# Moving transposes and gate products to later places in TensorE's queue: two layers of a diffusion trunk on one core

## The chip, the core and the metric

The kernel runs on one core of a Trainium2 chip. The metric is the device time of one execution, in microseconds; a change is judged by the median of several executions on the same chip. TensorE is written PE below (PEld for its weight loads), VectorE DVE, ScalarE ACT, GpSimd POOL and SyncE SP.

## What is computed

Two transformer layers over 512 latent tokens and 128 context tokens of width 1024, all in float32. The part of the reference that matters:

```python
def _layer(x, mod, p, lam_init, ctx):
    sh1, sc1, g1, sh2, sc2, g2 = mod
    h = _rmsnorm(x, p['norm1']) * (1.0 + sc1) + sh1
    m, new_ctx = _mixer(h, p, lam_init, ctx)
    x = x + g1 * m
    h = _rmsnorm(x, p['norm2']) * (1.0 + sc2) + sh2
    x = x + g2 * _conv_ffn(h, p)
    return x, new_ctx
```

The mixer projects h once and divides the columns among a bidirectional gated recurrence (RG-LRU, whose gates r and i are block products of the convolved input), grouped-query attention (q and k normalised per head, then rotated) and differential attention. Context tokens attend to context alone; latent tokens attend to the cached context keys and to themselves. The outputs are joined and projected back.

## The kernel before

**Tiling.** The 640 tokens are five tiles of 128: t = 0 to 3 latent, t = 4 context. Every float32 product is three products of rounded parts (mm3, L363 to L366: high by high, low by high, high by low), so one step over two k-blocks of one token tile is six matmuls. A layer runs: mixer (two LRU column blocks, then three projection groups `proj_group`, L633, of 4 weight blocks c times 5 token tiles; then the LRU gate columns), attention, output projection (`out_proj`), `ffn`.

**Who sets the order.** The schedule is manual: each engine gets its instructions in the order in which the Python program emits them. Work beside the products is put in by a small planner, `Flow` (L56). `fl.add(delay, fn, dve, need)` registers a function with a due time on the planner's own clock; `fl.step(ns)`, called after each step of products (1296 for a token tile of a group, 816 for two k-blocks of `stat_mm`), moves that clock and calls everything that is due, earliest due first. Some functions move the clock themselves (`fl.now += ...`) for the TensorE work that they put in. An item with a DVE cost is held while the planner's estimate of VectorE's backlog is over 1500, and an item with `need` waits for a free slot. These clock units are constants of the code, not measured times.

```python
GD = (5000, 1200, 11000, 2000)
CX = (3000, 4000, 4000, 3000, 6000, 12000, 8000)
NP = (1250, 4000, 950, 1700)
GQ = (5150, 3150, 2200, 1400)
```

**Queries.** `evac_gq` (L831), for each token tile of the first group: s1 (sums for the norm), s2 (scale and rotary, VectorE), s2b (rounding on GpSimd; needs one of two "st" slots), s3 (low part, L858, DVE), s4 (four transposes of a half into one PSUM bank, L867, and ScalarE's copies `qa`, L869; gives the slot back). The context tile takes c2 (L876) and c3 (four transposes `cqT`, L884). Key tiles take `k_stack` (L890): it needs an "st" slot too, and its `tr` (L902) puts in three transposes `kT`.

**Context attention.** `ctx_stage(n)` (L1049): four small score products `cS` (L1039) into two banks for n = 0, 1; row maxima on DVE (`cnm`, L1041); four exponentials on ACT (`cP`, L1044), which are the last readers of the two banks. Then `ctx_norm` and `ctx_T` (L1071, transposes `cPTp`). Stage 0 is due 12000 after the start of the third group, stage 1 20000 after it. The counter `pending["a"]` starts at 17 and falls with each s4 (8), key stack (5) and `ctx_T` (4); attention starts when it is 0.

**LRU gates.** `lru_gate` (L714): 16 products `gacc` (L722) for four calls, each followed by a sigmoid on ACT; due from 5000 on. They read xc, written by the convolution on DVE (L693, L696), and `lru_tail` (ACT, POOL, DVE) follows them.

**PSUM.** Outside attention there is one pool of eight banks (`pb`, L273). A bank goes to the next tile in the order in which banks were let go, and a tile that gets a used bank makes PE wait for the last reader of the old one. While a projection group runs, five banks hold its accumulators (one per token tile, `acc`), so that three go round among all transposes and small products.

**Norms.** `norm_pipe(t)` (L1323) is called as each tile of `out_proj` or `ffn` is finished: a (L1329: squares on ACT, then r and the scaled halves `xn` on POOL), 4000 later b (eight transposes `nT`, L569, into two banks, then `norm_c`: scale and shift on DVE and ACT, rounding `hi`, low part `lo`). The next stage starts with products over tiles 0 to 2 alone (384 columns, two weight blocks m of four pairs of k-blocks each), behind `need_h(0, 1, 2)` (L602), then goes on with tiles 3 and 4 (256 columns) behind `need_h(3, 4)`. There are three such joints: first out_proj to first ffn, first ffn to second mixer, second out_proj to second ffn.

Of the kernel before, what the change touches and what calls it, by code (L numbers as in the profile page):

```python
# [33 lines left out]
GD = (5000, 1200, 11000, 2000)  # L34
# [14 lines left out]
GQ = (5150, 3150, 2200, 1400)  # L49


def f32(ap):
    return ap.bitcast(F32)
# [179 lines left out]
def hybrid_kernel(ctx: ExitStack, tc: tile.TileContext, i, o):  # L233
# [13 lines left out]
    fl = Flow()  # L247
    fl.free["st"] = 2

    def half(name, dt=F32):  # L250
        return hpool.tile([128, 2 * W], dt, tag="h", name=name)

    def v2(t, n=W):
        return t.rearrange("p (a b) -> p a b", a=2)[:, :, :n]

    def tslot(name, n=644, dt=F32):
        return tp.tile([128, 644], dt, tag="t", name=name)[:, :n]
# [15 lines left out]
    def pb(name, dt=F32):  # L273
        return mode["pb"].tile([128, 512], dt, tag="pb", name=name)

    def pb2(name, cut=CH):

        return [pb(name), pb(name), cut]

    def small(name, n=8):  # L280
        return smp.tile([128, 8], F32, tag="sm", name=name)[:, :n]
# [86 lines left out]
    def round_pool(out, in_):  # L368
        pool.tensor_scalar(out=out, in0=in_, scalar1=1.0, scalar2=0.0, op0=ALU.mult, op1=ALU.add)
# [196 lines left out]
    def norm_b(n):  # L566
        pt = pb2("nT")
        for k in range(KD):
            pe.transpose(pt[k // 4][:, k % 4 * 128:k % 4 * 128 + 128], n[k // 4][:, k % 4 * 128:k % 4 * 128 + 128], ident)  # L569
        return pt  # L570
# [26 lines left out]
        fl.add(NP[2], hi)  # L597
        fl.add(NP[3], lo, 1340)

    h_left = set()  # L600

    def need_h(*tiles):  # L602
        while any(t in h_left for t in tiles):
            fl.step(200)

    def alloc_h():
        hh = [v2(half("hh", F32R), T) for _ in range(4)]
        hl = [v2(half("hl", F32R), T) for _ in range(4)]
        return hh, hl
# [38 lines left out]
    def mixer(l, hh, hl, first=None):  # L648
# [15 lines left out]
        kr, pending = [], {"t": 0.0, "lru": 2, "a": 17}  # L664
# [49 lines left out]
        def lru_gate(c, d):  # L714
            z = lru[c]
            if d == 0:
                z["gr"], z["gi"] = v2(half("lruR"), T), v2(half("lruI"), T)
            for t_, dst_ in ((0, z["gr"]), (1, z["gi"])):
                bc = R_GB + (l * 2 + d) * 4 + t_ * 2 + c
                for b in range(2):  # L720
                    acc, cs = pb("gacc"), slice(b * CH, b * CH + CH)
                    pe.matmul(acc[:, 0:CH], lhsT=z["gw"][:, d, t_], rhs=z["xc"][:, cs], start=True, stop=True)  # L722
                    act.activation(out=dst_[:, d, cs], in_=acc[:, 0:CH], func=ACTF.Sigmoid, bias=cols[:, bc:bc + 1])
            fl.now += 2150
# [95 lines left out]
        def head_rstd(src, nh):  # L820
            junk = tslot("hsq", nh * 64)
            act.activation(out=junk, in_=src, func=ACTF.Square)
            ss = small("hss", nh)
            dve.tensor_reduce(out=ss, in_=junk.rearrange("p (h d) -> p h d", d=64), op=ALU.add, axis=AX.X)
            return pow_rstd(ss, nh, 1.0 / 64)

        def scale_heads(src, r, nh):
            s3 = src.rearrange("p (h d) -> p h d", d=64)
            dve.tensor_tensor(out=s3, in0=s3, in1=r.unsqueeze(2).to_broadcast([128, nh, 64]), op=ALU.mult)

        def evac_gq(t, a):  # L831
            n = tslot("gqr", 512)
            act.activation(out=n, in_=a, func=ACTF.Copy)
            n3 = n.rearrange("p (h d) -> p h d", d=64)
            got = {}

            def s1():
                got["r"] = head_rstd(n, 8)
                if t < 4:
                    fl.add(GQ[1], s2, 2700)  # L840
                else:
                    fl.add(3500, c2, 1300)

            def s2():
                scale_heads(n, got["r"], 8)
                rope(n, t, rope_t["q"], 8, 64)
                for g in range(2):
                    fl.add(100, lambda g=g: s2b(g), 0, "st")

            def s2b(g):  # L850
                st = tslot("gqs", 512, F32R).rearrange("p (h s d) -> p h s d", h=4, s=2)
                hs = slice(4 * g, 4 * g + 4)
                round_pool(st[:, :, g], n3[:, hs])
                fl.add(GQ[2], lambda: s3(g, st), 350)

            def s3(g, st):
                hs = slice(4 * g, 4 * g + 4)
                dve.tensor_tensor(out=st[:, :, 1 - g], in0=n3[:, hs], in1=f32(st[:, :, g]), op=ALU.subtract)  # L858
                fl.add(GQ[3], lambda: s4(g, st))

            def s4(g, st):
                if not qa:
                    for p in range(4):
                        qa[p] = half("qa", F32R)[:, 0:1024].rearrange("p (h c) -> p h c", h=2)
                pt = pb("qT", F32R)
                for h in range(4):
                    pe.transpose(pt[:, h * 128:h * 128 + 128], st[:, h].rearrange("p s d -> p (s d)"), identr)  # L867
                for p in range(2):
                    act.activation(out=qa[2 * g + p][:, :, t * 128:t * 128 + 128],  # L869
                                   in_=f32(pt[:, p * 256:p * 256 + 256].rearrange("p (h c) -> p h c", h=2)),  # L870
                                   func=ACTF.Copy)
                fl.free["st"] += 1
                pending["a"] -= 1
                fl.now += 230

            def c2():  # L876
                scale_heads(n, got["r"], 8)
                dve.tensor_tensor(out=n3, in0=n3, in1=rope_t["qg"].unsqueeze(1).to_broadcast([128, 8, 64]), op=ALU.mult)
                fl.add(2500, c3)

            def c3():
                pt = pb("cqT")
                for b in range(4):
                    pe.transpose(pt[:, b * 128:b * 128 + 128], n[:, b * 128:b * 128 + 128], ident)  # L884
                act.activation(out=cqT, in_=pt[:, 0:512].rearrange("p (b c) -> p b c", b=4), func=ACTF.Copy)
                fl.now += 430

            fl.add(GQ[0], s1, 600)
# [141 lines left out]
        def ctx_probs(qT, kT, kd):  # L1030

            P = tslot("cP", 512).rearrange("p (n c) -> p n c", n=4)
            nm, den, rd = small("cnm", 4), small("cden", 4), small("crd", 4)
# [9 lines left out]
            for n in range(4):  # L1043
                act.activation(out=P[:, n], in_=blkof(n), func=ACTF.Exp, bias=nm[:, n:n + 1], accum_out=den[:, n:n + 1])  # L1044
            return P, den, rd

# [12 lines left out]
        def ctx_norm(n):  # L1059
            P, den, rd = ctxP[n]  # L1060
            dve.reciprocal(out=rd, in_=den)
            if n >= 2:
                for j in range(2):
                    dve.tensor_tensor(out=rd[:, 2 * j + 1:2 * j + 2], in0=rd[:, 2 * j + 1:2 * j + 2], in1=neglam[:, l:l + 1],
                                      op=ALU.mult)
            dve.tensor_tensor(out=P, in0=P, in1=rd.unsqueeze(2).to_broadcast([128, 4, 128]), op=ALU.mult)
            if n >= 2:
                dve.tensor_tensor(out=P[:, 0::2], in0=P[:, 0::2], in1=P[:, 1::2], op=ALU.add)
            fl.add(CX[3], lambda: ctx_T(n))

        def ctx_T(n):  # L1071
            P = ctxP[n][0]
            m = 4 if n < 2 else 2
            pt = pb("cPTp")
            for e in range(m):
                pe.transpose(pt[:, e * 128:e * 128 + 128], P[:, e if n < 2 else 2 * e], ident)
            dst = cPTg[:, 4 * n:4 * n + 4] if n < 2 else cPTd[n - 2]
            act.activation(out=dst, in_=pt[:, 0:m * 128].rearrange("p (n c) -> p n c", n=m), func=ACTF.Copy)
            fl.now += 430
            pending["a"] -= 1  # L1080
# [26 lines left out]
        rope_tables_()  # L1107
        for c in range(2):
            for d in range(2):
                fl.add(GD[0] + GD[1] * (2 * c + d), lambda c=c, d=d: lru_gate(c, d))  # L1110
        for c in range(2):
            fl.add(GD[0] + GD[2] + GD[3] * c, lambda c=c: lru_tail(c))
        proj_group(hh, hl, evac_gq)
# [209 lines left out]
    def norm_pipe(t, AB, h):  # L1323

        if not h:
            h.extend(alloc_h())
        h_left.add(t)
        box = {}

        def a():  # L1330
            sumsq(t, 1)
            box["n"] = norm_a(t)
            fl.add(NP[1], b)

        def b():
            pt = norm_b(box["n"])
            fl.now += 860
            A, B = AB()
            norm_c(t, pt, A, B, h[0], h[1])

        fl.add(NP[0], a)
# [309 lines left out]
```

## Time and profile before

| | us |
|---|---|
| median of 3 runs | 1639.22 (1639.19 to 1640.38) |
| the profiled execution's own time | 1639.05 |
| its span, first to last instruction | 1637.2 |
| PE busy in the span | 1589.8 |
| DVE busy | 943.5 |
| ACT busy | 722.7 |
| POOL busy | 351.2 |

Times in the rows are microseconds from the span's start. The page gives busy time of each engine, then the waits. A row of a wait names the engine, its line, "<-" and what released it, then the total, how often, and the longest. A timeline row has start, length, engine, line, operation, output<-input, how many instructions were merged, and in brackets the idle time before it and who ended it. The lengths of matmuls are modelled and overlap; the distance of two starts is what a matmul costs. PEclk is the clock granted to TensorE: 1.00 is 2.4 GHz, 0.50 is 1.2 GHz.

### The profile page before, as it was taken

To read this page: it belongs to the slowest core of one execution; us is meant where nothing else is said; L and a number is where in the kernel's file an instruction comes from. 1 tells how busy PE (TensorE), PEld (TensorE's weight loads), DVE (VectorE), ACT (ScalarE), POOL (GpSimd) and SP (SyncE) were. 2 spreads that over 40 slices of the span, in tenths; PEclk is the share of its full clock that TensorE was granted. 3 is DMA by queue.
4 is the path that set the end of the run, shared out by engine and by line. 5 is a ranking of instruction groups with operands and counts; after the bars stand their busy time and mean duration, and the time that the engine had idled before them with its cause. 6 is when DMAs were issued, how large, how long until landed. Compare 5 with 4: busy or idle time off the path is not lost. (4 is left out here: it accounts for less than half of the span.)

```text
span 1637.2 us, 25371 instructions
## 1 busy us (share of the span) xinstructions
PE 1589.8 (97%) x10070; PEld 1396.7 (85%) x10070; DVE 943.5 (58%) x1548; ACT 722.7 (44%) x1476; POOL 351.2 (21%) x782
## 2 busy tenths in 40 slices
PE   6999999999999999999999999999999999999998
PEld 4778776789999889999887787878899998899986
DVE  5687786465555434555467778765555553355544
ACT  4745777544333212333247367774433331133331
POOL 5162443032111000111052614420411100011101
PEclk9999999999999999999999999999999999999999
DMA  9222456412213221222312214352112232121312
GB/s 332 68 87 87 156 192 215 154 52 65 91 52 110 97 77 52 78 78 82 98 33 66 88 60 154 137 187 78 53 52 89 67 129 78 52 78 55 101 65 90
DMA packets 99434, 161.03 MB, mean 98 GB/s; under 512 B 10670, under 2 KB 69222, under 8 KB 94196
## 3 DMA queue, kind: packets, MB, share of 16 engines
q1 hardware_dynamic: 98068, 158.00, 28.9%
q8 instruction: 79, 1.29, 0.3%
q0 software_dynamic: 1040, 1.14, 0.2%
q14 instruction: 39, 0.32, 0.1%
q10 hardware_dynamic: 208, 0.28, 0.0%
HBM read 155.95 MB, written 3.44 MB: 97 GB/s over the span
## 5 line engine op out<-in xcount | busy, mean ns | idle before, releaser
L350 DVE TENSOR_TENSOR wl<-raw,wh 128x1024 fp32r<-128x1024 f32 x180 | 219.9, 1228 | 408.5 <-ACT wh L349 407.5
L365 PE MATMUL uacc<-hl,wh 128*128 128x320 f32 (+2 forms) x1408 | 437.3, 311 | 0.8 <-DVE hl L594 0.5
L364 PE MATMUL uacc<-hh,wh 128*128 128x320 f32 (+2 forms) x1408 | 437.4, 311 | 0.0
L366 PE MATMUL uacc<-hh,wl 128*128 128x320 f32 (+2 forms) x1408 | 435.1, 309 | 0.1
L349 ACT ACTIVATE wh<-raw 128x1024 fp32r<-128x1024 f32 x180 | 189.5, 1058 | 178.9 <-PE tacc L366 156.7
L365 PEld LDWEIGHTS uacc<-hl,wh 128*128 128x128 f32 x1408 | 265.2, 188 | 1.7 <-DVE hl L594 1.6
L366 PEld LDWEIGHTS uacc<-hh,wl 128*128 128x128 f32 x1408 | 265.9, 189 | 0.6 <-DVE wl L350 0.6
L364 PEld LDWEIGHTS uacc<-hh,wh 128*128 128x128 f32 x1408 | 265.5, 189 | 0.3
L364 PE MATMUL tacc<-wh,g 128*128 128x512 f32 x440 | 173.6, 395 | 0.0
L365 PE MATMUL tacc<-wl,g 128*128 128x512 f32 x440 | 173.6, 394 | 0.0
L366 PE MATMUL tacc<-wh,g 128*128 128x512 f32 x440 | 173.1, 393 | 0.0
L1369 POOL TENSOR_SCALAR ca<-u,fcol 128x642 f32<-128x642 f32 x44 | 38.9, 884 | 417.1 <-issue 244.4
L1161 DVE TENSOR_REDUCE nm<-S 128x1 f32<-128x640 f32 x128 | 101.7, 819 | 21.8 <-PE S L1151 11.4
L1176 POOL TENSOR_SCALAR P<-P,den 128x640 f32<-128x640 f32 x96 | 82.5, 865 | 143.4 <-DVE den L1170 77.2
L1165 ACT ACTIVATE P<-S,nm 128x640 f32<-128x640 f32 x128 | 100.8, 792 | 24.9 <-DVE nm L1161 21.4
L1365 ACT ACTIVATE u<-uacc 128x192 f32<-128x192 f32 (+1 forms) x88 | 29.0, 330 | 185.6 <-PE uacc L366 185.6
L366 PEld LDWEIGHTS tacc<-wh,g 128*128 128x128 f32 x440 | 82.7, 188 | 19.4
L364 PEld LDWEIGHTS tacc<-wh,g 128*128 128x128 f32 x440 | 82.6, 188 | 19.3
L365 PEld LDWEIGHTS tacc<-wl,g 128*128 128x128 f32 x440 | 82.7, 188 | 18.9
L364 PE MATMUL acc<-wh,hh 128*128 128x512 f32 x240 | 97.0, 404 | 0.0
L366 PE MATMUL acc<-wh,hl 128*128 128x512 f32 x240 | 95.4, 397 | 0.0
L365 PE MATMUL acc<-wl,hh 128*128 128x512 f32 x240 | 95.2, 397 | 0.0
(292 smaller groups left out, 2667.9 us busy)
## 6 DMA issues: line engine op xcount, KB each, us to landing
raw<-in_ffn_w_up_dram SPq DMA_DIRECT2D x44, 1024.0 KB, 5.1
raw<-in_ada_w_dram SPq DMA_DIRECT2D x40, 1024.0 KB, 4.9
raw<-in_ffn_w_down_dram SPq DMA_DIRECT2D x20, 1024.0 KB, 5.0
raw<-in_w_in_dram SPq DMA_DIRECT2D x16, 1024.0 KB, 8.4
araw<-in_ada_w_dram SPq DMA_DIRECT2D x16, 512.0 KB, 9.5
raw<-in_w_out_dram SPq DMA_DIRECT2D x8, 1024.0 KB, 6.6
gates<-gate SPq DMA_DIRECT2D x8, 512.0 KB
x<-in_x_sample_dram SPq DMA_DIRECT2D x4, 512.0 KB
```

The costliest lines, as they stand in the source:

```text
L349: act.activation(out=wh, in_=raw, func=ACTF.Copy)
L350: dve.tensor_tensor(out=wl, in0=raw, in1=f32(wh), op=ALU.subtract)
L364: pe.matmul(out, lhsT=lh, rhs=rh, start=start, stop=False)
L365: pe.matmul(out, lhsT=lh, rhs=rl, start=False, stop=False)
L366: pe.matmul(out, lhsT=ll, rhs=rh, start=False, stop=stop)
L1161: dve.tensor_reduce(out=box["nm", c], in_=view(c), op=ALU.max, axis=AX.XY, negate=True)
L1165: act.activation(out=box["P"][c].rearrange("p (a b) -> p a b", a=2), in_=view(c), func=ACTF.Exp, bias=box["nm", c], accum_out=box["den"][: ...
L1176: pool.tensor_scalar(out=P[-1], in0=P[-1], scalar1=den[:, 1 + comps:2 + comps], scalar2=0.0, op0=ALU.mult, op1=ALU.add)
L1365: act.activation(out=u[:, 1 + cut:1 + L], in_=acc[1][:, 0:L - cut], func=ACTF.Copy)
L1369: pool.tensor_scalar(out=out, in0=u[:, 1:1 + n], scalar1=wcol(1), scalar2=wcol(3), op0=ALU.mult, op1=ALU.add)
```

## The change

It moves work to later places in the order of emission; no instruction is added or taken away. The s4 of token tile 3 is due 1500 later, the transposes of the context queries (c3) 2000 later, the gates of the first layer 2200 later. A `ctx_T(n)` that comes due while more than 4 - n of the 17 items are open is put off by 300. In the norms, b of tiles 3 and 4 is put off by 300 as long as its tile is in `h_late`, which the first `need_h` of the next stage empties as it returns.

```diff
@@ -597,11 +597,15 @@
         fl.add(NP[2], hi)
         fl.add(NP[3], lo, 1340)
 
-    h_left = set()
+    h_left, h_late = set(), set()
 
     def need_h(*tiles):
+
+        if 4 in tiles:
+            h_late.clear()
         while any(t in h_left for t in tiles):
             fl.step(200)
+        h_late.clear()
 
     def alloc_h():
         hh = [v2(half("hh", F32R), T) for _ in range(4)]
@@ -856,7 +860,7 @@
             def s3(g, st):
                 hs = slice(4 * g, 4 * g + 4)
                 dve.tensor_tensor(out=st[:, :, 1 - g], in0=n3[:, hs], in1=f32(st[:, :, g]), op=ALU.subtract)
-                fl.add(GQ[3], lambda: s4(g, st))
+                fl.add(GQ[3] + 1500 * (t == 3), lambda: s4(g, st))
 
             def s4(g, st):
                 if not qa:
@@ -876,7 +880,7 @@
             def c2():
                 scale_heads(n, got["r"], 8)
                 dve.tensor_tensor(out=n3, in0=n3, in1=rope_t["qg"].unsqueeze(1).to_broadcast([128, 8, 64]), op=ALU.mult)
-                fl.add(2500, c3)
+                fl.add(4500, c3)
 
             def c3():
                 pt = pb("cqT")
@@ -1069,6 +1073,8 @@
             fl.add(CX[3], lambda: ctx_T(n))
 
         def ctx_T(n):
+            if pending["a"] > 4 - n:
+                return fl.add(300, lambda: ctx_T(n))
             P = ctxP[n][0]
             m = 4 if n < 2 else 2
             pt = pb("cPTp")
@@ -1107,7 +1113,7 @@
         rope_tables_()
         for c in range(2):
             for d in range(2):
-                fl.add(GD[0] + GD[1] * (2 * c + d), lambda c=c, d=d: lru_gate(c, d))
+                fl.add(GD[0] + 2200 * (l == 0) + GD[1] * (2 * c + d), lambda c=c, d=d: lru_gate(c, d))
         for c in range(2):
             fl.add(GD[0] + GD[2] + GD[3] * c, lambda c=c: lru_tail(c))
         proj_group(hh, hl, evac_gq)
@@ -1325,6 +1331,8 @@
         if not h:
             h.extend(alloc_h())
         h_left.add(t)
+        if t > 2:
+            h_late.add(t)
         box = {}
 
         def a():
@@ -1333,6 +1341,8 @@
             fl.add(NP[1], b)
 
         def b():
+            if t in h_late:
+                return fl.add(300, b)
             pt = norm_b(box["n"])
             fl.now += 860
             A, B = AB()
```

## Rows read from the trace of the kernel before

**Rows 1.** The page, busy time of each engine in the whole span.

```profile
PE 1589.8 (97%) x10070; PEld 1396.7 (85%) x10070; DVE 943.5 (58%) x1548; ACT 722.7 (44%) x1476; POOL 351.2 (21%) x782
```

**Rows 2.** Waits of PE: waiter, releaser, total us, times, longest.

```profile
PE nT L569 <- POOL xn L563: 2.5, 5, 1.3
PE qT L867 <- DVE gqs L858: 2.4, 2, 1.2
PE gacc L722 <- issue: 1.7, 1, 1.7
PE cqT L884 <- DVE gqr L878: 1.6, 2, 0.8
```

**Rows 3.** Timeline of PE, end of the second projection group, first layer.

```profile
113.58 0.87 PE L867 MATMUL qT<-identr,gqs 128*128 128x128 f32 x8 [1.17 <-DVE gqs L858]
115.25 0.66 PE L884 MATMUL cqT<-ident,gqr 128*128 128x128 f32 x4 [0.79 <-DVE gqr L878]
115.66 0.48 PE L364 MATMUL acc<-wh,hh 128*128 128x512 f32 x1
```

**Rows 4.** Stretches: us, busy (count) of PE, PEld, DVE, ACT, POOL; PEclk; DMA.

```profile
76.00:112.00 36.00, 36.00 (x156) 29.09 (x155) 35.41 (x47) 15.87 (x24) 21.96 (x21) 1.00 0.22 68
112.00:116.00 4.00, 2.04 (x16) 1.44 (x15) 3.93 (x7) 2.38 (x10) 0.49 (x1) 1.00 0.78 278
...
916.00:920.00 4.00, 1.97 (x16) 1.61 (x16) 3.93 (x7) 2.62 (x10) 0.25 (x1) 0.99 0.75 265
920.00:923.40 3.40, 3.40 (x10) 2.66 (x9) 0.99 (x5) 1.22 (x5) 2.62 (x7) 0.51 0.00 0
...
302.00:305.60 3.60, 3.17 (x8) 2.51 (x9) 1.50 (x2) 1.55 (x2) 0.00 (x0) 0.53 0.20 35
835.80:839.00 3.20, 1.25 (x9) 0.83 (x9) 2.77 (x5) 1.56 (x5) 3.06 (x4) 1.00 0.00 0
```

**Rows 5.** Timeline of DVE and of PE around the first layer's gates.

```profile
56.13 1.01 DVE L696 SCALAR_TENSOR_TENSOR lruG<-lruX,cols 128x512 f32<-128x512 f32 x2
...
57.09 7.24 PE L722 MATMUL gacc<-lruG,lruW 128*128 128x320 f32 x26 [1.74 <-issue]
```

**Rows 6.** Timeline of PE and of ACT, first ffn to second mixer.

```profile
837.25 0.66 PE L569 MATMUL nT<-ident,xn 128*128 128x128 f32 x4 [1.26 <-POOL xn L563]
838.60 0.66 PE L569 MATMUL nT<-ident,xn 128*128 128x128 f32 x4 [0.69 <-POOL xn L563]
839.01 0.42 PE L364 MATMUL lacc<-hh,wh 128*128 128x384 f32 x1
...
844.54 0.66 PE L569 MATMUL nT<-ident,xn 128*128 128x128 f32 x4
...
840.73 0.64 ACT L549 ACTIVATE sqj<-x 128x512 f32<-128x512 f32 x1
```

**Rows 7.** Timeline of PE, then of ACT, third projection group, first layer.

```profile
132.87 0.80 PE L867 MATMUL qT<-identr,gqs 128*128 128x128 f32 x8
133.60 1.18 PE L1039 MATMUL cS<-cx 64*128 64x128 f32 x8
134.72 0.50 PE L364 MATMUL acc<-wh,hh 128*128 128x512 f32 x1
...
143.82 0.72 PE L1039 MATMUL cS<-cx 64*128 64x128 f32 x8
...
135.14 1.28 ACT L1044 ACT_TABLE_LOAD   x1 [0.56 <-DVE cnm L1041]
136.44 0.37 ACT L1044 ACTIVATE cP<-cS,cnm 128x128 f32<-128x128 f32 x1
...
137.39 0.20 ACT L1044 ACTIVATION_READ_ACCUMULATOR cP<-cS,cnm 128x1 f32 x1
...
146.04 0.21 ACT L1044 ACTIVATION_READ_ACCUMULATOR cP<-cS,cnm 128x1 f32 x1
```

**Rows 8.** Instructions of the tile cS: idle time of an engine, by releaser.

```profile
  ACT qa L869: 0.4, 2
```

## The prediction

> **What bounds the kernel now.** I read the busy times first: PE works through 1589.8 of 1637.2 us [rows 1], so a microsecond is won or lost only where PE's queue stands still. The list of PE's waits came next; four of its rows belong to the parts that the change moves: 2.5 us at norm transposes, 2.4 us at query transposes, 1.7 us at a gate product, 1.6 us at the context queries' transposes [rows 2], 8.2 us or 0.5% together. Then the timeline at these waits, to see what PE would do if the waiting instruction stood elsewhere, and the stretches, to see whether another engine is full there. The last thing I read was the third projection group, where PE hardly waits, because the moved query transposes land there. The profiled execution took 1639.05 us, its span and 1.85 us around it; the median is 0.17 us above it. Sums are made against 1639.05 and given out with 0.17 added. A measurement of this kernel tells about 0.2% from no change, 3.3 us, so the bounds are 1635.9 and 1642.5.
>
> **Context queries, c3 (twice).** Before, half-stacks of tile 0 and the context transposes stand side by side in PE's queue: the first start at 113.58 after a wait, the others at 115.25 after another, and products go on at 115.66 [rows 3]. Eight such transposes cost 0.73 us where nothing waits (132.87 to 133.60 [rows 7]), so without c3 the products would go on at 114.31, 1.35 us earlier. The planner puts c3 two token steps later, where its input has long been written; there it costs its own 0.41 us (115.25 to 115.66) and about 0.1 for refilling the pipeline: net 0.85 us per layer, **-1.7**. The wait of 1.17 us ahead of it stays, because it belongs to tile 0, which the change does not move.
>
> **The clock in the second layer.** At the same place in the second layer PE idled in the same manner, and right behind it the granted clock stood at 0.51 for 3.4 us, the 1.2 GHz level; in the first layer it stayed at 1.00 [rows 4]. Half speed for 3.4 us loses some 1.6 us. With one of the two waits gone I count this fall as gone: **-1.6**; if it stays, 0.
>
> **Gates, first layer.** PE waits 1.74 us at the first gate product, and xc is written by two DVE instructions from 56.13, 1.01 us long together, just ahead of it [rows 5]; the planner puts the gates two token steps later (six instead of four behind the group's start), 2 x 6 x 0.23 us (36.00 us for 156 products in [rows 4]) = 2.8 us, so this wait is gone. But the recurrence starts only behind the sigmoids, and DVE is busy for 35.41 of the next 36.00 us [rows 4]: PE arrives earlier at tile 0's query transposes and waits there for DVE as much longer. I take **0**; the ends are -1.9 (all kept) and +0.2.
>
> **Norms, three joints.** First ffn to second mixer: the two halves of tile 3's transposes wait 1.26 and 0.69 us for POOL [rows 6]. Put behind one pair of k-blocks, they still end when POOL lets them, but the pair is done by then: five pairs take 5.5 us (839.01 to 844.54), so 1.1 us is won. Tile 4's squares, behind tile 3's scaling on ACT until 840.73, move ahead of it, so its transposes and the low parts behind them wait less; an estimate of 0.3. **-1.4**, ends -2.4 and -0.5. At the other two joints tile 3 hardly waits, and b of tile 4 comes one pair earlier than its POOL halves allow: up to 1.1 us lost at the transposes, and about as much regained, because the 256-column products behind find their low parts ready. **0**, ends -0.5 and +0.5 each.
>
> **Query transposes of tile 3 (twice).** This is the part that decides. By the planner's arithmetic s3 of tile 3 runs 9126 units into the third group (six steps of 1296, four s4 of 230 and 430 for the context keys), so s4 is due at 10526 before and at 12026 after. Context stage 0 is due at 12000. Before, s4 runs in the step at 11718, moves the clock by 2 x 230, and the stage follows in the same step: transposes at 132.87, scores at 133.60, no product between them [rows 7]. After, both come due in the step at 13014, and the stage, 26 units earlier, goes **first**. Three banks go round here. Before, the stage's second bank was the first transposes' bank, and PE shows it: the scores last 1.18 us, where the next stage's last 0.72 [rows 7], and the releaser is ACT's query copy [rows 8]. After, the order is score bank 1, score bank 2, transposes g = 0, transposes g = 1; the fourth needs the first bank, whose last reader is the third exponential. That one ended at 137.59 (137.39 + 0.20), 3.99 us behind the scores' start, 0.46 of it their own wait: 3.5 to 3.7 us, taken as 3.6, through row maxima and a table load of 1.28 us. PE gets to g = 1 after 0.65 + 0.37 = 1.0 us, waits 2.6, and needs 0.37 more: 4.0 us until products go on, against 1.85 before (132.87 to 134.72). All products of the core stand behind that transpose. +2.1 per layer, **+4.2**. That ACT's query copies queue behind the exponentials costs nothing: nothing reads them before attention.
> On the load, ACT goes from it to the exponential in 0.02 us (135.14 + 1.28 to 136.44 [rows 7]). The Trainium skill, "ScalarE: Activation LUTs", section "What ACT_TABLE_LOAD costs", adds a drain of about 1.38 us to each load; by that figure, an estimate, the sum would be 2.8 us higher, and the row shows no such piece behind the load.
>
> **Key stacks, pushed by the same delay (twice).** They need the slots that s4 gives back, so their first transposes slip from the step after stage 0 into the step of context stage 1 (due at 20000, step at 20854; they are due at 20858, and the stage moves the clock by 900). The order there is score bank 1, score bank 2, keys of tile 0, keys of tile 1, and again the fourth waits for the third exponential: 146.25 against 143.82, 2.4 us without a load [rows 7], of which PE fills 0.9. +1.5 per layer, **+3.0**; 0 if they miss that step. The deferred context transposes (`ctx_T`) follow behind the last keys, beside the gate-column products, where their ACT inputs are ready: 0.
>
> **New falls of the clock.** PE standing for 2.6 us is of the size that went with a fall before: 0.53 behind the start of the output projection, 0.51 in the second layer, none in the first layer or at the joint (1.26 + 0.69 us idle) [rows 4, 6]. I take one at each long wait: 2 x 1.6 = **+3.2**; ends 0 and +4.8.
>
> **Sum.** -1.7 - 1.6 + 0 - 1.4 + 0 + 4.2 + 3.0 + 3.2 = +5.7: 1644.75 for the profiled execution, **1644.9** for the median.
>
> **Rivals.**
> 1. *The three banks are enough* (faster): the scores do not precede the transposes, or their banks come free in time, and both bank waits and their clock falls are missing: -4.7, 1634.5. For it: hardly a wait of PE is listed in the third group now, and 0.46 us is all that bank reuse costs there. Against it: the 26 units, and the row that shows the reuse order. The Trainium skill, "Perfetto Trace Analysis", section "Optimizing Tensor Performance", says that groups rotating through different banks let one's evacuation overlap the next one's products. By it this rival would hold; the row with the 0.46 us shows a rotation that is already too short.
> 2. *Only the first bank wait comes* (no change): the key transposes fall into a step of their own. -3.0, and one clock fall rather than two: 1640.3; with both falls 1641.9, with none 1638.7.
> 3. *The gates' 1.7 us is kept*, if the DVE chain starts earlier with PE. Against it: DVE's full stretch. It would take 1.7 off any case: 1643.2 for the forecast.
>
> **How the numbers follow.** The forecast's case gets 0.60: the order follows from constants, the length of the wait from rows; its own range is 1641 to 1647.5 (no to three clock falls, norms at either end). Rival 1 gets 0.18, rival 2 0.17, rival 3 alone 0.05. The range 1636.0 to 1647.5 holds the forecast's case, rivals 2 and 3, and leaves out most of rival 1 and the dearest end, under 0.2. Faster by over 0.2%: nearly all of rival 1, 0.17. Within 0.2%: rival 2, the forecast's case without a clock fall (1641.7, about 0.08) and a little of the rest, 0.25. Slower: 0.58.
>
> **What would show it.** In the third group of each layer, scores `cS` ahead of tile 3's `qT`; the last four `qT` starting 2.5 to 3 us behind them, released by ACT's exponentials `cP`; another such gap of 1.5 us between two `kT`; PEclk near 0.5 behind the long gaps. The gate wait gone and the wait at tile 0's `qT` in the first layer grown; `cqT` without a wait; one pair of `lacc` products ahead of `nT` at 836 us. If `qT` stands before `cS`, or starts right behind it, the main step is wrong, and the time is near 1634.5.

## The result, and the profile after

The changed kernel took 1647.99 us (median of 4 runs, 1646.47 to 1651.66) against 1639.2 us before. The ratio on record is 1.0059, with a 95% interval of 1.0047 to 1.0071 (the two medians alone give 1.0054). Measured again, on another chip, the ratio was 1.0067 (1.0054 to 1.0080). It is slower by 0.6%. The prediction had the sign and the main mechanism, but 1644.9 us was 3.1 us short, and its range ended 0.5 us below the measurement.

The profiled execution took 1646.62 us, 7.57 more than the 1639.05 of before. The page still shows PE full, with less work time than in [rows 1] and a longer span (1644.8 us), so the loss is time in which PE's queue stood:

```profile
PE 1588.1 (97%) x10070; PEld 1394.4 (85%) x10070; DVE 943.3 (57%) x1548; ACT 722.7 (44%) x1476; POOL 351.8 (21%) x782
```

The list of PE's waits of the changed kernel (who waits, for whom, total us, times, longest) answers to [rows 2]. `gacc` and `cqT` are gone from it, `nT` fell from 2.5 to 2.0, and five rows at the moved transposes are new:

```profile
PE qT L871 <- ACT cP L1048: 5.2, 2, 2.6
...
PE kT L909 <- DVE kr L821: 2.9, 2, 1.4
...
PE nT L569 <- POOL xn L563: 2.0, 2, 1.1
PE cPTp L1082 <- DVE cP L1072: 1.8, 2, 0.9
...
PE kT L909 <- DVE gks L902: 1.1, 2, 0.6
...
PE cPTp L1082 <- ACT lrug L708: 0.9, 2, 0.4
```

To see where the time went, I laid the two timelines of PE side by side and took the difference of start times, after minus before, at instructions that both have (the times in brackets are those of before):

| first layer, at | us | second layer, at | us |
|---|---|---|---|
| first projection group (49.55) | +0.1 | first projection group (855.77) | +2.8 |
| tile 0's query transposes (113.58) | +0.1 | tile 0's query transposes (917.35) | +2.8 |
| products behind `cqT` (118.75) | -0.9 | products behind `cqT` (924.09) | +0.3 |
| products behind tile 3's `qT` (139.01) | +3.1 | products behind tile 3's `qT` (943.41) | +4.1 |
| `cdkT` (154.94) | +4.1 | `cdkT` (960.34) | +5.1 |
| first score of attention (172.51) | +6.8 | first score of attention (977.88) | +7.9 |
| output projection (301.38) | +5.4 | output projection (1099.67) | +7.3 |
| eight products later (305.56) | +3.9 | | |
| behind the first joint's norms (377.19) | +4.2 | behind the third joint's norms (1173.20) | +7.6 |
| behind the second joint's norms (850.72) | +3.0 | late in the second ffn (1526.29) | +7.6 |

Three jumps repeat in both layers: 3.9 us around tile 3's transposes, 1.0 us from there to `cdkT`, and 2.7 us from `cdkT` to attention. The timeline of PE in the first layer's third group, and behind it, shows what they are made of (start, length, instruction, count, idle time before it and its releaser):

```profile
133.57 0.72 PE L1043 MATMUL cS<-cx 64*128 64x128 f32 x8
134.22 0.53 PE L871 MATMUL qT<-identr,gqs 128*128 128x128 f32 x4
137.37 0.51 PE L871 MATMUL qT<-identr,gqs 128*128 128x128 f32 x4 [2.62 <-ACT cP L1048]
146.37 0.71 PE L1043 MATMUL cS<-cx 64*128 64x128 f32 x8
147.02 0.45 PE L909 MATMUL kT<-identr,gks 128*128 128x128 f32 x3
148.90 0.42 PE L909 MATMUL kT<-identr,gks 128*128 128x128 f32 x3 [1.43 <-DVE kr L821]
...
166.06 0.28 PE L909 MATMUL kT<-identr,gks 128*128 128x128 f32 x1 [0.56 <-DVE gks L902]
167.13 0.60 PE L1082 MATMUL cPTp<-ident,cP 128*128 128x128 f32 x4
167.66 0.50 PE L1043 MATMUL cS<-cx 32*128 32x128 f32 x8
168.61 0.66 PE L1082 MATMUL cPTp<-ident,cP 128*128 128x128 f32 x4 [0.44 <-ACT lrug L708]
...
177.49 0.41 PE L1082 MATMUL cPTp<-ident,cP 128*128 128x128 f32 x2 [0.92 <-DVE cP L1072]
179.30 0.42 PE L1156 MATMUL S<-kk,qa 128*128 128x320 f32 x1 [0.53 <-ACT lrug L708]
```

Against [rows 7] the scores now stand ahead of tile 3's transposes, and the second four of these wait. ACT's timeline there shows the table load, and the third exponential from 136.82 to 137.18, 0.19 us ahead of the released transposes:

```profile
134.82 1.28 ACT L1048 ACT_TABLE_LOAD   x1 [6.14 <-DVE cnm L1045]
136.12 0.37 ACT L1048 ACTIVATE cP<-cS,cnm 128x128 f32<-128x128 f32 x1
...
136.82 0.36 ACT L1048 ACTIVATE cP<-cS,cnm 128x128 f32<-128x128 f32 x1
```

Stretches of that place (us; busy us and count of PE, PEld, DVE, ACT, POOL; PEclk; DMA) show PE idle for two whole microseconds and then at the 1.2 GHz level, as [rows 4] had it at other places:

```profile
135.00:137.00 2.00, 0.00 (x0) 0.00 (x0) 1.86 (x9) 1.99 (x6) 0.40 (x1) 1.00 0.01 4
137.00:139.00 2.00, 1.63 (x9) 1.48 (x10) 1.86 (x7) 2.00 (x9) 1.06 (x2) 0.94 0.00 0
139.00:141.00 2.00, 2.00 (x6) 1.53 (x6) 1.52 (x3) 0.66 (x1) 0.00 (x0) 0.50 0.00 0
141.00:143.00 2.00, 2.00 (x8) 1.58 (x7) 1.90 (x8) 0.00 (x0) 0.00 (x0) 0.71 0.50 98
```

### The profile page after: what moved, and what is told of

It is laid out like the page before. It is cut to its first block, busy times and chain, and to the rows that moved or that the text cites. A ratio compares the mean times of both kernels' runs of the same rounds, so it can differ in the third digit from the quotient of the medians.

```text
span 1644.8 us, 25371 instructions
## 1 busy us (share of the span) xinstructions
PE 1588.1 (97%) x10070; PEld 1394.4 (85%) x10070; DVE 943.3 (57%) x1548; ACT 722.7 (44%) x1476; POOL 351.8 (21%) x782
## 4 chain that ended last, share of the span: by engine, by line
PE 82%; DVE 8%; ACT 5%; POOL 2%; DMA 1%; issue 1%; SPq 1%; DVEq 0%; POOLq 0%; ACTq 0%
PE uacc L365 12%; PE uacc L364 12%; PE uacc L366 12%; PE tacc L365 8%; PE tacc L366 8%; PE tacc L364 8%; PE PT L1191 3%; PE PV L1216 3%; PE ada L507 2%; PE acc L364 2%; PE acc L365 2%; PE acc L366 2%; PE S L1161 1%; DVE wl L350 1%; PE S L1156 1%
```

## The experiments

The times of before in each group are from the same chip: 1637.43 us for the first four runs, 1638.26 for the next four, 1639.09 for the last four.

### Which parts cost: without the delay (e2), and without its guard too (e1)

```diff
-                fl.add(GQ[3] + 1500 * (t == 3), lambda: s4(g, st))
+                fl.add(GQ[3], lambda: s4(g, st))
...
-            if pending["a"] > 4 - n:
-                return fl.add(300, lambda: ctx_T(n))
```

> The changed kernel without the 1500 units on tile 3's query transposes and without the guard in ctx_T: the later context queries, the later gates and the norm part are left. Theory A (all of the loss comes from the delay and its guard): the other three parts keep what the trace of the changed kernel shows for them, -0.93 at cqT in each layer, -1.6 for the clock fall behind it in the second layer, -1.2 at the second joint, +0.2 at each of the other two, 0 for the gates: -4.3, about 1635 us, ratio near 0.9974. Rival B (the three parts cost something themselves, by clock falls or the norms): no faster than before, 1638 us or more.

Measured 1633.41 us, ratio 0.9975 (0.9965 to 0.9985): 4.0 us under before, where theory A had 4.3. The other three parts are a gain, and all of the loss sits in the delay and its guard.

The same with the guard kept (first line of the diff alone):

> As the run without delay and guard, but with the guard in ctx_T kept, so that the context transposes of stages 0 and 1 still go behind the last keys. Theory A1 (the waits in the gate-column products, 0.44 us for the recurrence's ACT work and 0.92 us for the norm of stage 3 in each layer, come from the guard): 1.4 us dearer per layer than without it, about +2.8 us, 1637.8 us. Rival (they come from the delay, which pushes everything behind it): same as without the guard within 0.5 us.

Measured 1633.16 us, ratio 0.9972 (0.9962 to 0.9982). Theory A1 is wrong in this form: by itself the guard costs nothing. The last key stack and the eight context transposes stand behind `cdkT` there too, in one piece ahead of stage 2, and wait for nobody. The products from `cdkT` to attention take 18.29 us in the first layer instead of 17.57 before, and those ahead of `cdkT` about 0.5 us less: the work has moved, and hardly any time is lost.

### The delay and guard alone (e12)

The kernel before, with these two edits and nothing else.

> The kernel before with tile 3's delay of 1500 and the guard in ctx_T alone. Theory (the parts add up): the changed kernel stands 10.7 us above before and the run without delay and guard 4.0 below, so these two cost some 14.7 us: ratio 1.008 to 1.010, with the waits of 2.62 us (qT, for the third exponential) and 1.43 us (kT) in both layers. Rival (the cost comes from the parts together, as the context queries of c3 are moved too): ratio 1.005 or less.

Measured 1653.76 us against 1639.09, ratio 1.0093 (1.0077 to 1.0108): +14.7 us, as the sum of the parts had it. Its list of waits has the two bank waits to the tenth, beside the old waits at `gacc` and `cqT`:

```profile
PE qT L867 <- ACT cP L1044: 5.2, 2, 2.6
...
PE kT L905 <- DVE kr L817: 2.9, 2, 1.4
```

### Lateness or order (e3)

```diff
-                fl.add(GQ[3] + 1500 * (t == 3), lambda: s4(g, st))
+                fl.add(GQ[3] + 1450 * (t == 3), lambda: s4(g, st))
```

> The changed kernel with 1450 instead of 1500 units: the transposes still come one token step later than before, but by the planner's arithmetic ahead of context stage 0, and the first keys ahead of stage 1. Bank-order theory: the waits of 2.62 us (qT) and 1.43 us (kT) and the clock fall of 1.6 us go in each layer, 0.5 us for the second score bank comes back in each: some -10 us against the changed kernel, about 1637 us (the guard's cost stays). Rival (the lateness itself costs, whatever the order): within 2 us of the changed kernel, 1645 to 1648 us.

Measured 1635.91 us, ratio 0.9987 (0.9978 to 0.9996). Fifty units of the planner's clock are worth 11 to 12 us, since the changed kernel's ratios of 1.0059 and 1.0067 are 1647 to 1648 us on this chip. PE's timeline has the same transposes just as late, but ahead of the scores, and the first keys ahead of stage 1:

```profile
133.46 0.80 PE L871 MATMUL qT<-identr,gqs 128*128 128x128 f32 x8
134.19 1.20 PE L1043 MATMUL cS<-cx 64*128 64x128 f32 x8
142.37 0.62 PE L909 MATMUL kT<-identr,gks 128*128 128x128 f32 x6
...
143.66 0.71 PE L1043 MATMUL cS<-cx 64*128 64x128 f32 x6 [0.25 <-ACT kl L914]
...
158.05 0.37 PE L909 MATMUL kT<-identr,gks 128*128 128x128 f32 x3
158.35 0.50 PE L1043 MATMUL cS<-cx 32*128 32x128 f32 x8
158.78 1.09 PE L1082 MATMUL cPTp<-ident,cP 128*128 128x128 f32 x8
```

The scores last 1.20 us again, with the 0.46 us for the query copy inside them, as in [rows 7]. From `cdkT` to attention this kernel loses 0.6 us against before (the differences of start times are -0.73 and -0.11), where the changed kernel loses 2.7. It stands 2.5 us above the run without delay and guard; what lateness alone costs is no more than that.

### Is it the bank (e4)

```diff
-            for n in range(4):
+            for n in ((0, 2, 1, 3) if banks == 2 else range(4)):
                 act.activation(out=P[:, n], in_=blkof(n), func=ACTF.Exp, ...
```

> The changed kernel, with the four exponentials of context stages 0 and 1 in the order 0, 2, 1, 3, so that the first score bank is read out by the second exponential instead of the third. Bank theory: the wait of qT falls from 2.62 by one exponential's spacing of 0.35 us to about 2.27 us, and that of kT from 1.43 to about 1.08 us, in both layers: 1.4 us in all, with clock falls as they come. Rival for kT, where the trace names a DVE rotation of keys as releaser (kr): kT's wait stays at 1.43 us and only qT's falls, 0.7 us in all.

Measured 1647.32 us, ratio 1.0057. The time can't show 1.4 us here, but the list of waits does: 2.62 went to 2.27 (4.5 in two), 1.43 to 1.07 (2.1 in two).

```profile
PE qT L871 <- ACT cP L1048: 4.5, 2, 2.3
...
PE kT L909 <- DVE ropet L818: 2.1, 2, 1.1
```

Both transposes wait for the exponential that empties the first score bank. For `kT` the trace names an instruction of DVE that ended near it, `kr` in one kernel and `ropet` in this one; in the second measurement of the changed kernel the same wait carries the other name:

```profile
149.74 0.42 PE L909 MATMUL kT<-identr,gks 128*128 128x128 f32 x3 [1.42 <-ACT cP L1048]
```

### The changed kernel again (e5)

> The changed kernel once more, beside the kernel before, because its four runs lay between 1646.5 and 1651.7 us. Theory (the spread is that of the clock falls, which differ from execution to execution): about +9 us against before, ratio 1.004 to 1.007, a spread of 3 to 5 us again, and the profiled execution shows some other places of the falls than 138.8 and 944 us besides the waits' own. Rival (the first four runs were unlucky): ratio near 1.0035, as the sum of the prediction has it.

Measured 1648.92 us (1647.99 to 1650.12), ratio 1.0067. The rival is out, but the theory was not right in all: the spread was 2.1 us instead of 3 to 5, and the falls of the profiled execution stand at the same two waits as before, not at other places. It has the same waits; the clock stood at the lower level for 6.8 us from 136 on, over the end of the wait and almost six microseconds of products, and again for 3.4 us at 945. In the two rows below (same columns as above) the level is reached before PE starts again:

```profile
135.00:137.00 2.00, 0.00 (x0) 0.00 (x0) 1.83 (x9) 1.99 (x8) 0.40 (x1) 0.79 0.02 4
137.00:139.00 2.00, 1.83 (x7) 1.67 (x8) 1.90 (x6) 2.00 (x8) 1.06 (x2) 0.50 0.00 0
```

### What makes the last stretch ahead of attention dear (e6, e9)

First, stage 0 without its 900 units on the planner's clock:

```diff
-            fl.now += 900
+            fl.now += 900 * (n > 0)
```

> The changed kernel, but context stage 0 does not move the planner's clock (900 units for stage 0 left out): scores still come ahead of tile 3's query transposes, but these run 900 units earlier by the planner, and give their slots back to the keys as much earlier; the first keys then stand ahead of stage 1. Theory (planner push: the waits in the key stacks and in the gate-column products are there because stage 0 pushes the transposes and with them the key stacks a step back): qT's wait of 2.62 us and its clock fall stay, kT's 1.43 us goes, and of the 1.9 us of waits in the gate-column products most goes: 2.5 to 3.3 us per layer, 5 to 6.5 us in all, about 1641 us. Rival (these waits come from the delay itself or from the guard): kT's 1.43 us alone goes, 3 us in all, 1644 us.

Measured 1647.84 us, ratio 1.0049 (1.0035 to 1.0062), only 1.1 us under the changed kernel of the same chip. The keys did move ahead of stage 1, and the wait of 1.43 us went; but from `cdkT` to attention it still loses 2.15 us against before (differences +4.27 and +6.42). Of the three waits in that stretch the two at `cPTp` (0.44 and 0.92 us) are gone, as the theory had it, but the wait of the last keys is still 0.59 us, those at `cdkT` and at the first score are 0.3 us longer each, and the stretch is only 0.56 us shorter than in the changed kernel. So the late last keys don't come from the 900 units, and the theory of a push by the planner's clock held for the first keys and not for the time of that stretch.

Second, the guard one looser, which changes nothing up to the fourth key stack:

```diff
-            if pending["a"] > 4 - n:
+            if pending["a"] > 5 - n:
```

> The changed kernel with the guard in ctx_T one looser (5 - n instead of 4 - n): everything up to the fourth key stack keeps its order, but the context transposes of stages 0 and 1 go ahead of the last keys again instead of behind them. Theory (guard on top of the late keys): the waits of 0.45 us (recurrence's ACT work) and 0.93 us (norm of stage 3) that the gate-column products show in each layer go with their refills, the gate-column products up to attention take 1.4 to 2 us less per layer: about 3 to 4 us less than the changed kernel, 1645 us. Rival (the last keys alone, whose low parts are late by 0.56 us, push what is behind them): no more than 0.5 us per layer less.

Measured 1647.41 us against 1639.09, ratio 1.0045 (1.0033 to 1.0058). The trace decides it. Up to `cdkT` this kernel stands where the changed kernel stood (+4.0, with the wait of 2.62 us at 136.93), but from there to attention it loses 0.28 us in the first layer and 0.26 in the second, instead of 2.7 in each:

```profile
154.79 0.62 PE L1082 MATMUL cPTp<-ident,cP 128*128 128x128 f32 x4
158.95 0.44 PE L1028 MATMUL cdkT<-ident,cdk 128*128 128x128 f32 x2 [0.75 <-ACT cdk L1021]
161.90 0.60 PE L1082 MATMUL cPTp<-ident,cP 128*128 128x128 f32 x4
...
164.72 0.37 PE L909 MATMUL kT<-identr,gks 128*128 128x128 f32 x3
...
175.62 0.38 PE L1082 MATMUL cPTp<-ident,cP 128*128 128x128 f32 x2
```

No wait is left at `cPTp` or at the last `kT`. Four context transposes stand ahead of `cdkT` again, which makes that stretch 0.3 us longer than in the changed kernel. Both stretches together, from behind tile 3's `qT` to attention, are 1.6 us longer than before in each layer, where the changed kernel has 3.7: the looser guard is worth 2.1 us per layer. That the median fell by less than these 4.2 us has a cause in the same trace: its clock fell five times 3.4 us, against three in the changed kernel's run above. The delay without any guard was not tried.

### Does the clock fall because PE stands (e10)

```diff
-                for h in range(4):
+                for h in list(range(4)) * (6 if t == 3 and g == 0 else 1):
                     pe.transpose(pt[:, h * 128:h * 128 + 128], ...
```

> The changed kernel, with the transposes of tile 3, g = 0, done six times over (20 more in each layer, writing the same values to the same bank), so that PE works through most of the wait for the score bank. The wait's end stays where ACT puts it. Theory (the clock falls behind the two long waits because PE stands): no fall near 136 to 147 us and near 944 us in the trace, 1.6 to 2.4 us less in each layer, 3 to 4 us in all. Rival (falls come by themselves): falls at these places as before, the time within 1 us of the changed kernel or above it.

Measured 1650.39 us, ratio 1.0065 (1.0051 to 1.0078): nothing won. The fall at this place did go, but another came behind the next long wait, that of `kT`. PE's timeline, where the wait ends 3.16 us behind the first transposes' start as in the changed kernel (3.15), and three stretches (the trace puts the wait down to POOL, but the third exponential ended at 137.04, again 0.19 us ahead of the released transposes):

```profile
134.07 2.23 PE L871 MATMUL qT<-identr,gqs 128*128 128x128 f32 x24
137.23 0.51 PE L871 MATMUL qT<-identr,gqs 128*128 128x128 f32 x4 [0.93 <-POOL gks L369]
```

```profile
137.00:139.00 2.00, 1.77 (x10) 1.58 (x11) 1.90 (x6) 2.00 (x9) 1.06 (x2) 1.00 0.00 0
146.00:148.00 2.00, 0.78 (x4) 0.76 (x5) 1.90 (x8) 1.99 (x11) 0.41 (x1) 0.87 0.00 0
148.00:150.00 2.00, 2.00 (x6) 1.57 (x5) 0.92 (x3) 1.94 (x5) 0.00 (x0) 0.50 0.00 0
```

In the second layer the fall stands behind the wait of `kT` as well (959.8). Each theory got half: with the wait filled no fall comes at that place, but taking one occasion away doesn't take the loss away.

### The other parts (e7, e8), and a try for more (e11)

The norm part alone (the delay, the guard, `c3` and the gates as before), and the norm part with `c3` at 4500:

> The kernel before with the norm part alone. Theory (the trace of the changed kernel, joint by joint): +0.2, -1.2, +0.2, with the clock fall in the second layer still there: -0.8 us, within 0.1% of before. Rival (the two halves of tile 4's transposes cost more at joints where POOL is behind): +0.5 us or more.

> The kernel before with the norm part and the later context queries (c3 at 4500), gates as before. Theory: another 0.93 us less in each layer and the clock fall behind the second layer's wait gone, -1.9 to -3.5 us against the norm part alone, about 0.2% under before; equal to the run without delay and guard within 0.5 us, since the gates give back what they win. Rival (the gates keep their 1.7 us): 1.7 us dearer than the run without delay and guard.

The norm part alone took 1635.96 us, ratio 0.9988 (0.9979 to 0.9997): 2.3 us less, more than the 0.8 expected. Its trace has -1.2 us at the second joint and about +0.3 at each of the others, so the rest is not the norms'. In the profiled execution 1.6 us of it is the clock fall of the second layer: it did not come, although both waits ahead of it (1.27 and 0.79 us) are there as before. Here is the stretch with both waits, with the clock at its upper level throughout:

```profile
915.00:924.00 9.00, 8.13 (x47) 6.82 (x48) 5.21 (x13) 6.24 (x22) 5.07 (x12) 1.00 0.17 54
```

With `c3` it took 1634.17, ratio 0.9979 (0.9970 to 0.9988): 1.8 us less, 0.9 per layer. That is 4.1 us under before, and the run with the gates as well had 4.0: the gates give back what they win.

> The kernel before with the norm part and the later context queries, and three stack slots instead of two in the planner, so that queries and keys are transposed earlier and more apart. Theory: the wait at tile 0's query transposes (1.17 us in the kernel before) stays, key stacks come earlier, no bank wait: 0 to 1.5 us less than with two slots, about 0.3% under before. Rival (more stacks in flight meet the full stretch of DVE, or tiles run out): slower than with two slots by 1 us or more.

The planner's `fl.free["st"] = 2` made 3, on top of the norm part and `c3`: 1642.08 us, ratio 1.0015 (1.0006 to 1.0025), slower. The rival was right that it loses. The profiled execution was the fastest of the eleven (1638.26 us), so it shows only part of the loss. Key stacks come so early in it that a bank wait is back (PE's row, then ACT's):

```profile
138.99 0.77 PE L909 MATMUL kT<-identr,gks 128*128 128x128 f32 x6 [1.53 <-POOL gks L369]
...
138.43 0.37 ACT L1048 ACTIVATE cP<-cS,cnm 128x128 f32<-128x128 f32 x1
```

The trace puts this wait down to POOL's rounding, but that ended at 138.42 (138.01 + 0.41), 0.57 us earlier. The third exponential of stage 0, in the second row, ended at 138.80, 0.19 us ahead of the transposes, as at the bank waits above; one key stack had taken the third bank, and these transposes are the fourth in turn.

The version to keep is the change without tile 3's delay: 0.9972 of the time before with the guard and 0.9975 without it, equal within their intervals.

## Why the prediction was off

**The order of scores and transposes: right.** The 26 units put stage 0 first, the second four transposes waited 2.62 us (2.6 predicted) for the third exponential, and a clock fall came behind: 3.9 us per layer at the next products, 3.7 predicted (2.1 and a fall of 1.6). Run e3, with 1450, and run e4, with the exponentials' order, show both halves of the argument, the order and the bank. The exponential followed the table load after 0.02 us once more (134.82 + 1.28 to 136.12). The Trainium skill, "ScalarE: Activation LUTs", section "What ACT_TABLE_LOAD costs", adds a drain to each load; the measured wait has no room for it.

**Rival 1: wrong, by the same runs.** The Trainium skill, "Perfetto Trace Analysis", section "Optimizing Tensor Performance", has groups in different banks overlap. With three banks going round that held for one order (1450: 0.46 us at the scores) and not for the other (1500: 2.62 and 1.43 us): here rotation helped as far as the reader of the oldest bank was done.

**Key stacks: right.** The wait was 1.43 us, 1.5 predicted. The stretch up to `cdkT` grew by 1.0 us only, because four context transposes and a key stack had left it for the next one. With the context transposes back in it (e9) the two stretches together are 1.6 us longer than before.

**Deferred context transposes, "where their ACT inputs are ready: 0": this step failed.** They cost 2.1 us in each layer, 4.2 together (e9 against the changed kernel), more than the whole miss. The jump of 2.7 us from `cdkT` to attention holds this, and besides it some 0.6 us of transposes that only moved there. I looked at the transposes' own inputs and counted the move as free. What I left out is what stands beside and behind them: with the last keys late as well, keys, two sets of transposes and stage 3 came in a row in the last products ahead of attention. PE waited 0.56 us for a low part of the keys, and 0.44 for the recurrence's work on ACT; that can only be for a bank, since `cPTp` reads nothing of `lrug`. It waited 0.92 at the end for the norm of a stage that had started 5 us later (167.66 against 162.57 before). In the kernel before, the transposes and the stage of this stretch show no idle time ahead of them:

```profile
156.11 0.60 PE L1076 MATMUL cPTp<-ident,cP 128*128 128x128 f32 x4
...
162.57 0.50 PE L1039 MATMUL cS<-cx 32*128 32x128 f32 x8
```

Run e9 takes away the deferral and with it these waits; run e2 shows that the guard does no harm where the keys come earlier. So the loss belongs to the guard and the late keys together. Why the last keys come later than with 1450 stays open: e6 shows only that it isn't stage 0's 900 units.

**Gates: 0, right, but in another place.** PE came 1.7 us early out of the gates, and was back at +0.1 by tile 0's transposes. Most of it went not there, as I had said, but earlier, in two waits for DVE's low parts of weights; tile 0's wait grew by 0.19 only, against [rows 3]:

```profile
80.94 0.50 PE L365 MATMUL acc<-wl,hh 128*128 128x512 f32 x1 [0.67 <-DVE wl L350]
...
109.46 0.50 PE L365 MATMUL acc<-wl,hh 128*128 128x512 f32 x1 [0.32 <-DVE wl L350]
...
113.65 0.88 PE L871 MATMUL qT<-identr,gqs 128*128 128x128 f32 x8 [1.36 <-DVE gqs L862]
```

**Context queries: right.** -0.93 us per layer, -0.85 predicted, and no wait at `cqT`.

**Norms: right in size, at the second joint not in the working.** The second joint gave -1.2 us (-1.4 predicted), the others +0.2 and +0.3 (0). The prediction had tile 3's transposes still waiting for POOL, with a pair of products done ahead of them. In the trace these transposes wait for nobody, and the pair itself waits, 1.12 us for ACT's rounding and 0.56 for DVE's low part, nearly as long as the transposes had waited before (1.26 and 0.69 [rows 6]); that the size came out near is luck in part:

```profile
841.30 0.45 PE L364 MATMUL lacc<-hh,wh 128*128 128x384 f32 x1 [1.12 <-ACT hh L589]
842.31 0.44 PE L365 MATMUL lacc<-hl,wh 128*128 128x384 f32 x1 [0.56 <-DVE hl L594]
```

**Clock: right in the profiled execution's places, too small over all executions.** In that execution the fall of the second layer went and two came behind the long waits, as predicted. That the first went because a wait went is not shown: the norm part alone (e7) has both waits and no fall there either.

**What hid the loss.** The fall at 302 us [rows 4] went too, 1.4 us that I had not counted on, and 1.9 us came back in attention. Of these, 1.4 us belong to the first layer, where matmuls wait for weights by DMA: at the one place where PE had waited 0.70 and 0.92 us for them before (270 and 274 us) it now waits 0.27. The 0.5 us of the second layer I can't explain. Neither gain is shown to belong to the change. Ten of the fourteen traces have a fall between 299 and 308 us, though the second one of the changed kernel has none either. At those weights e9's trace has 0.66 and 0.64 us again, and e7's 0.97, where its order is still that of before: such a wait differs from execution to execution. Together they hid 3.3 of the 4.2 us of the failed step: 5.7 + 4.2 - 3.3 = 6.6, and small differences at all the other places (+0.3 us at most each) add 1.0, for 7.57 measured. Other executions were dearer: the median lies 1.4 us above the profiled one, and one run of 1651.66 us had a mean granted clock of 0.992 instead of 0.997.

## What to carry to other kernels

Where a planner issues by due times, a delay that lands close to another due time (here 26 units in 12000) can be a change of order: work out which comes first, then follow the buffers round, and move it clear of the tie. A deferred step is free only if what queues behind it is covered too; here the last products ahead of attention did not cover it. In a full kernel, the gains of a change are worth timing part by part, since two small ones here (norms and `c3`) were hidden by one loss.

## What the runs showed of the hardware

The clock falls follow long waits, but not one to one. Each fall to 1.2 GHz lasted 3.4 us, or 6.8, which I count as two (the last microseconds of the span left out). The seven traces with the scores ahead of tile 3's transposes (the changed kernel, e5, e4, e6, e9, e10, e12) show 2, 3, 3, 6, 5, 5 and 4 of them, 4.0 on average; the seven others (before, e1, e2, e3, e7, e8, e11) show 2, 1, 0, 2, 2, 3 and 1, 1.6 on average. Of the 28 falls of the first set, 14 stand at the waits for a score bank, 8 at the start of the output projection (305 to 308 us), where 6 of the 11 of the second set stand as well (299 to 302), and 4 at 842 to 847 us, where these kernels wait no more than others with the norm part. Of the second set, one stands behind e11's bank wait. At about 1.6 us each, 2.4 more is some 4 us, an estimate from these counts, where the prediction had a net of 1.6. Filling the wait moved a fall to the next wait (e10), and the same two waits had a fall in the kernel before and none in e7. What decides at which wait a fall comes, these runs do not show.

A bank wait carries several names in these traces. The transposes that waited for the third exponential started 0.19 us behind its end in the changed kernel, in e10 and in e11, and the releaser named was ACT's `cP`, DVE's `kr` or `ropet`, or POOL's `gks`.
